# A 90-degree rotation of an 8192 x 8192 matrix: the tile scheduler's unrolled program is replaced by hand-placed buffers, a chunk grid and a PE loop of 64 transposes

## The chip, the cores and the metric

The kernel runs on one core of a Trainium2 chip. The core has five engines that matter here: TensorE (PE, which also does the transposes), VectorE (DVE), ScalarE (ACT), GpSimd (POOL) and SyncE (SP, which here only issues transfers). Sixteen DMA engines move data between the device memory (HBM) and the on-chip memory (SBUF); TensorE writes its results to PSUM, from where another engine has to copy them to SBUF. The metric is the time of one execution on the device in microseconds (us), lower is better. Of the kernel before there are three timed runs: 1267.24, 1267.49 and 1268.66 us, median 1267.49 us.

## The reference

```python
def setup_inputs():
    return {
        "x": np.random.randn(8192, 8192).astype(np.float32),
        "k": 1,
    }

def reference(x, k):
    return np.rot90(x, k)
```

Nothing is computed: row `i` of the output is column `8191 - i` of the input. The 268.4 MB of the input are read once and 268.4 MB of output are written once. The work is a transpose of every 128 x 128 block with the columns in reversed order.

## The kernel before

The input is cut into macro tiles of 1024 rows by 4096 columns (`R = 1024`, `W = 4096`): eight row bands with two macro tiles each. The last macro tile is cut in two of 512 rows (`LAST = [4, 4]`). A macro tile is loaded by `load` in eight transfers of 128 rows x 4096 columns (2 MB each, 16 KB in one piece per row), issued on SP's queue (L102). Every landed row block is copied by VectorE in eight copies of 128 x 512 (L108); each copy also reverses the columns inside each 128-wide block, and puts the result in one of 63 small buffers (`r_pool`). A load buffer is free for the next load when its eight copies are done.

`store` then makes the output of a macro tile in eight units of 2 MB. For a unit, TensorE does 32 transposes of 128 x 128 (L148: the chunk is the loaded operand, the identity matrix the other) into two PSUM tiles of 128 x 2048 (two such tiles exist, together all of PSUM). ScalarE copies each PSUM tile to half of an output buffer (L169), and then issues the store of the whole unit on its own queue (L177): 512 output rows, 4 KB of each.

The buffers are pools: two buffers of 16 KB per partition for loads (`a_pool`), three for stores (`o_pool`), 63 chunk buffers of 2 KB. During the first macro tile, when nothing is stored yet, `load` borrows the store buffers too (`loads % 5 >= 2`), so that five loads are under way. Near the end `store` borrows the load buffers (`end and i % 2 == 0`). Two units of the first macro tile (`i in (4, 6)`) and the last unit of all are stored in two halves. The first unit of a macro tile is transposed row block by row block as the chunks arrive; the others block column by block column. The last half macro tile is loaded while the one before it is stored.

The order on each engine's queue, and every wait, comes from the tile scheduler, which derives them from the order of the calls and from the pools. Each engine's program is straight-line code: TensorE's holds 4096 transposes, each with its own load of the operand. Every engine works through its own queue in order; an instruction waits for the semaphores that the scheduler gave it.

Of the kernel before, what the change touches and what calls it, by code (L numbers as in the profile page):

```python
# [2 lines left out]

# [5 lines left out]

P = 128  # L10

R = 1024
RT = R // P
LAST = [4, 4]
W = 4096
CH = 512
F = 4096  # L20
FP = 2048


def whole_reads(nc):

    for fn in nc.m.functions:
        for block in fn.blocks:
            for n, ins in enumerate(block.instructions):
                if not isinstance(ins, mybir.InstDMACopy):
                    continue
                src = ins.ins[0]
                ap = [list(d) for d in src.ap]
                if len(ap) == 3 and ap[2][0] == 1 and ap[1][0] == ap[2][1]:
                    ap = [ap[0], [1, 1], [1, ap[1][1] * ap[2][1]]]
                    block.instructions[n] = copy.replace(  # L40
                        ins,
                        ins=[copy.replace(src, ap=ap)],
                        ant_dge_precooked=False,
                    )


def macro_tiles(N, M):

    tiles = [(r0, RT, c0) for r0 in range(0, N, R) for c0 in range(0, M, W)]
    r0, _, c0 = tiles.pop()  # L50
    for n in LAST:
        tiles.append((r0, n, c0))
        r0 += n * P
    return tiles


@with_exitstack
def kernel(
    ctx: ExitStack,
    tc: tile.TileContext,  # L60
    x: bass.AP,
    k: bass.AP,
    out: bass.AP,
):
    nc = tc.nc
    assert k == 1, f"only k=1 supported, got {k}"
    nc.at_finalize(whole_reads)

    N, M = x.shape
    dt = x.dtype  # L70

    consts = ctx.enter_context(tc.tile_pool(name="consts", bufs=1))
    ident = consts.tile([P, P], dt)
    make_identity(nc, ident)

    a_pool = ctx.enter_context(tc.tile_pool(name="a_pool", bufs=2))
    r_pool = ctx.enter_context(tc.tile_pool(name="r_pool", bufs=63))
    o_pool = ctx.enter_context(tc.tile_pool(name="o_pool", bufs=3))
    psum_pool = ctx.enter_context(
        tc.tile_pool(name="psum", bufs=2, space=bass.MemoryType.PSUM)  # L80
    )

    loads = 0

    def load(r0, rt, c0):

        nonlocal loads
        chunks = {}
        for t in range(rt):


            if loads < RT and loads % 5 >= 2:
                a = o_pool.tile([P, W], dt, tag="o")
            else:
                a = a_pool.tile([P, W], dt, tag="a")  # L100
            loads += 1
            nc.sync.dma_start(  # L102
                out=a[:], in_=x[r0 + t * P : r0 + (t + 1) * P, c0 : c0 + W]
            )
            yield chunks
            for j in range(W // CH):
                ar = r_pool.tile([P, CH // P, P], dt, tag="ar")
                nc.vector.tensor_copy(  # L108
                    out=ar[:],
                    in_=a[:, j * CH : (j + 1) * CH].rearrange(  # L110
                        "r (b m) -> r b m", m=P
                    )[:, :, ::-1],
                )
                chunks[t, j] = ar
            yield chunks

    def store(r0, rt, c0, chunks, end):

        rows = rt * P
        PW = 1
        while 2 * PW * rows <= FP:
            PW *= 2
        G = PW
        while 2 * G * rows <= F:
            G *= 2
        for i, g0 in enumerate(range(0, W // P, G)):  # L130
            if end and i % 2 == 0:
                ot = a_pool.tile([P, F], dt, tag="a")
            else:
                ot = o_pool.tile([P, F], dt, tag="o")
            o = ot[:, : G * rows].rearrange("m (g f) -> m g f", g=G)

            lead = r0 == 0 and c0 == 0 and i in (4, 6)
            S = PW if lead or (end and r0 + rows == N and g0 + G == W // P) else G  # L140


            ps = {}

            def transposes(t, ws):
                for w in ws:
                    g = g0 + w
                    nc.tensor.transpose(  # L148
                        ps[w // PW][:, PW - 1 - w % PW, t * P : (t + 1) * P],
                        chunks[t, g * P // CH][:, g % (CH // P), :],  # L150
                        ident,
                    )

            def psum_tile(h):
                pt = psum_pool.tile([P, FP], mybir.dt.float32, tag="ps")
                ps[h] = pt[:, : PW * rows].rearrange("m (g f) -> m g f", g=PW)

            if i == 0 and (rt == RT or r0 + rows < N):
                for h in range(G // PW):
                    psum_tile(h)  # L160
                for t in range(rt):
                    transposes(t, range(G))
            for h in range(0, G, PW):
                if h // PW not in ps:
                    psum_tile(h // PW)
                    for w in range(h, h + PW):
                        for t in range(rt):
                            transposes(t, [w])
                nc.scalar.copy(o[:, G - PW - h : G - h, :], ps[h // PW])  # L169

                done = h + PW
                if done % S == 0:
                    top = M - c0 - (g0 + done) * P
                    dst = out[top : top + S * P, r0 : r0 + rows].rearrange(
                        "(g m) f -> m g f", g=S
                    )
                    nc.scalar.dma_start(  # L177
                        out=dst, in_=o[:, G - done : G - done + S, :]
                    )
            yield  # L180

    tiles = macro_tiles(N, M)
    *most, before_last, last = tiles
    for m in most:
        *_, chunks = load(*m)
        for _ in store(*m, chunks, False):
            pass


    *_, chunks = load(*before_last)  # L190
    outputs = store(*before_last, chunks, True)
    rows = load(*last)
    for _ in range(2 * last[1] - 1):
        next(rows)
    next(outputs)
    chunks = next(rows)
    for _ in outputs:
        pass
    for _ in store(*last, chunks, True):
        pass  # L200


# [1 line left out]
_INS = ['x', 'k']  # L204
_OUTS = [((8192, 8192), 'float32')]

_NUMBERS = {'k': 1}


# [26 lines left out]
```

## Time and profile before

| | before |
|---|---|
| median of three runs | 1267.49 us |
| the profiled execution: span | 1266.1 us |
| median less span | 1.39 us |
| DMA: moved, mean rate | 537.55 MB, 425 GB/s |
| PE busy (transposes) | 718.2 us, 57% |
| ACT busy (PSUM to SBUF) | 466.7 us, 37% |
| DVE busy (chunk copies) | 355.4 us, 28% |
| granted TensorE clock, mean | 0.762 |

The profile is one execution recorded by the hardware profiler. The span goes from the first to the last recorded instruction. "Busy" is the time in which an engine had at least one instruction under way; register, semaphore and DMA-issuing instructions do not count. A line such as `L169 ACT COPY ot<-pt` names the source line, the engine, the operation and what is written from what. Idle time is given with what ended it: `<-DMA out_dram<-ot` means that a landed store released the engine. The DMA row of the time slices is the mean busy share of the sixteen DMA engines, in tenths.

### The profile page before, as it was taken

The numbers are of one execution on the slowest core, as the hardware profiler recorded it, in microseconds if no ns is written. First come the engines' busy times: TensorE is split into PE (matmuls) and PEld (weight loads), VectorE is DVE, ScalarE is ACT, GpSimd is POOL, SyncE is SP. The second block draws the span as 40 slices with busy tenths as digits, with TensorE's granted clock in tenths as the row PEclk, the third lists the DMA queues.
The fourth block names the chain that finished last, engine by engine and source line by source line (L and its number), as shares of the span: only waits on it lengthen the run. The fifth ranks groups of instructions, "written<-read, shape, count | busy, mean of one in ns | idle before, by whom it ended". The sixth has DMA issues, their size and how long they took to land.

```text
span 1266.1 us, 10392 instructions
## 1 busy us (share of the span) xinstructions
PE 718.2 (57%) x4096; PEld 678.6 (54%) x4096; DVE 355.4 (28%) x1024; ACT 466.7 (37%) x257; POOL 0.7 (0%) x6
## 2 busy tenths in 40 slices
PE   1554565556656665556555665555655656556673
PEld 1543455555555555456554655555655655556562
DVE  4423223222232223222232223322232222322210
ACT  0432433433333333343334333343333433343363
POOL 0000000000000000000000000000000000000000
PEclk9977877777776777867778678677686686776797
DMA  9999999999999999999999999999999999999997
GB/s 399 426 428 430 428 429 427 430 429 429 429 429 429 430 428 427 430 429 430 428 430 428 429 429 428 430 428 428 430 430 428 429 429 428 428 428 428 427 399 328
DMA packets 37345, 537.55 MB, mean 425 GB/s; under 512 B 4144, under 2 KB 4144, under 8 KB 4144
## 3 DMA queue, kind: packets, MB, share of 16 engines
q10 hardware_dynamic: 18864, 268.44, 50.0%
q1 hardware_dynamic: 18432, 268.44, 49.7%
q8 instruction: 32, 0.52, 0.2%
q14 instruction: 17, 0.14, 0.0%
HBM read 268.44 MB, written 268.44 MB: 424 GB/s over the span
## 4 chain that ended last, share of the span: by engine, by line
DMA 82%; ACT 14%; PE 1%; issue 1%; ACTq 1%; DVE 0%; SPq 0%
DMA out_dram<-ot 79%; ACT ot L169 14%; DMA a<-in_x_dram 3%; PE pt L148 1%; ACTq L177 0%; DVE ar L108 0%; ACTq L169 0%; SPq L102 0%
## 5 line engine op out<-in xcount | busy, mean ns | idle before, releaser
L148 PE MATMUL pt<-ident,ar 128*128 128x128 f32 x4096 | 718.2, 356 | 528.0 <-ACT ot L169 487.6
L148 PEld LDWEIGHTS pt<-ident,ar 128*128 128x128 f32 x4096 | 678.6, 191 | 567.4 <-ACT ot L169 521.4
L169 ACT COPY ot<-pt 128x2048 f32<-128x2048 f32 x256 | 465.4, 1869 | 756.7 <-DMA out_dram<-ot 727.0
L108 DVE COPY ar<-a 128x512 f32<-128x512 f32 x1024 | 355.4, 421 | 861.1 <-DMA a<-in_x_dram 524.0
L169 ACT ACT_TABLE_LOAD x1 | 1.3, 1283 | 25.5 <-DVE ar L108 25.5
masks.py:199 POOL TENSOR_SCALAR_AFFINE_SELECT ident<-ident 128x128 f32<-128x128 f32 x1 | 0.3, 292 | 0.1
masks.py:197 POOL MEMSET ident<- 128x128 f32 x1 | 0.2, 204 | 0.3 <-POOLq L217 0.3
L217 POOL MEMSET const-bfloat16-1.0<- 128x1 bf16 x1 | 0.1, 102 | 0.0
L217 POOL MEMSET const-uint8-127<- 128x1 uint8 x1 | 0.1, 102 | 0.0
L217 POOL MEMSET const-float32-0.0<- 128x1 f32 x1 | 0.1, 99 | 0.2 <-issue 0.2
L217 POOL MEMSET const-float32-1.0<- 128x1 f32 x1 | 0.1, 99 | 0.0
## 6 DMA issues: line engine op xcount, KB each, us to landing
a<-in_x_dram SPq DMA_DIRECT2D x128, 2048.0 KB, 16.8
out_dram<-ot ACTq DMA_DIRECT2D x125, 2048.0 KB, 25.5
out_dram<-ot ACTq DMA_DIRECT2D x6, 1024.0 KB, 27.3
```

The costliest lines, as they stand in the source:

```text
L108: nc.vector.tensor_copy(out=ar[:], in_=a[:, j * CH : (j + 1) * CH].rearrange("r (b m) -> r b m", m=P)[:, :, ::-1],)
L148: nc.tensor.transpose(ps[w // PW][:, PW - 1 - w % PW, t * P : (t + 1) * P], chunks[t, g * P // CH][:, g % (CH // P), :], ident,)
L169: nc.scalar.copy(o[:, G - PW - h : G - h, :], ps[h // PW])
L217: nc = _bacc.Bacc("TRN2", target_bir_lowering=False, num_devices=1)
```

## The change

The kernel is written without the tile scheduler. All buffers have fixed addresses and all semaphores are written out.

- There are four 16 KB buffers (`bufs`). Loads use all four during the first macro tile and then buffers 0 and 1; stores use buffers 2 and 3, and all four for the last eight units. So there are two buffers for loads and two for stores, where there were two and three.
- The 63 chunk buffers become one grid of 8 x 8 chunks of 128 x 512 (`grid`, 128 KB per partition). VectorE first copies a landed row block whole (128 x 4096, in order) into a row or a column of the grid (`place`). For an output unit it then gathers, four times, the eight 128 x 128 blocks of one block column, with reversed columns, into one of two stages of 4 KB per partition (`stage`). When a unit's four gathers are done, its eight chunks of the grid are free, and VectorE places the row block that came eight loads later there; so rows and columns of the grid change roles from one macro tile to the next.
- TensorE runs a loop: 64 iterations of 64 transposes from the two stages to fixed PSUM addresses. Before each group of eight it waits for a full stage (`s_full`), before every second group also for a free half of PSUM (`s_free`). After each group it raises `s_pe`, which frees the stage.
- ScalarE copies each half of PSUM and then waits for its own copy (`s_act`) before it gives the half back. It issues every unit's store whole. The macro tiles are all of 1024 rows, and no store is split.
- A `Block` puts a barrier of all engines before and after this part.

```diff
-R = 1024
-RT = R // P
-LAST = [4, 4]
-W = 4096
-CH = 512
-F = 4096
-FP = 2048
+R = 1024
+T = R // P
+W = 4096
+G = 4
+J = W // (G * P)
+CH = G * P
+F = G * R
+LOOP = 8
+PAIR = 2
...
-    a_pool = ctx.enter_context(tc.tile_pool(name="a_pool", bufs=2))
-    r_pool = ctx.enter_context(tc.tile_pool(name="r_pool", bufs=63))
-    o_pool = ctx.enter_context(tc.tile_pool(name="o_pool", bufs=3))
...
+    macros = [(r0, c0) for r0 in range(0, N, R) for c0 in range(0, M, W)]
+    n_out = len(macros) * J
+    n_load = len(macros) * T
+
+    with tc.tile_critical():
+        ident = nc.alloc_sbuf_tensor("ident", [P, P], dt)
+        bufs = [nc.alloc_sbuf_tensor(f"buf{i}", [P, F], dt) for i in range(4)]
+        grid = nc.alloc_sbuf_tensor("grid", [P, T * J * CH], dt)
+        stage = [nc.alloc_sbuf_tensor(f"stage{i}", [P, R], dt) for i in range(2)]
+        ps = nc.alloc_psum_tensor("ps", [P, 4 * R], mybir.dt.float32)
...
+        def load_buf(m):
+            return m % 4 if m < T else m % 2
+
+        def out_buf(n):
+            return 2 + n % 2 if n < n_out - J else (2 + n) % 4
+
+        def slots(t, kk):
+            g = grid[:].rearrange("p (a b c) -> p a b c", a=T, b=J)
+            return g[:, t, :, :] if kk % 2 == 0 else g[:, :, t, :]
+
+        def column(j, kk):
+            g = grid[:].rearrange("p (a b c) -> p a b c", a=T, b=J)
+            return g[:, :, j, :] if kk % 2 == 0 else g[:, j, :, :]
...
+            @block.sync
+            def _(e):
+                last = {}
+                for m in range(n_load):
+                    b = load_buf(m)
+                    if b in last:
+                        e.wait_ge(s_copy, last[b] + 1)
+                    last[b] = m
+                    r0, c0 = macros[m // T]
+                    r0 += m % T * P
+                    e.dma_start(
+                        out=bufs[b][:], in_=x[r0 : r0 + P, c0 : c0 + W]
+                    ).then_inc(s_land[b], 16)
+
+            @block.vector
+            def _(e):
+                def place(m):
+                    b = load_buf(m)
+                    e.wait_ge(s_land[b], land_wait[m])
+                    e.tensor_copy(
+                        out=slots(m % T, m // T),
+                        in_=bufs[b][:].rearrange("p (j c) -> p j c", c=CH),
+                    ).then_inc(s_copy, 1)
+
+                for t in range(T):
+                    place(t)
+                for n in range(n_out):
+                    kk, j = divmod(n, J)
+                    for w in range(G):
+                        g = n * G + w
+                        if w == 0:
+                            e.wait_ge(s_copy, T * (kk + 1))
+                        if g >= 2:
+                            e.wait_ge(s_pe, g - 1)
+                        e.tensor_copy(
+                            out=stage[g % 2][:].rearrange("p (t c) -> p t c", c=P),
+                            in_=column(j, kk)[:, :, w * P : (w + 1) * P][:, :, ::-1],
+                        ).then_inc(s_full, 1)
+                    if n + T < n_load:
+                        e.drain()
+                        place(n + T)
+
+            @block.tensor
+            def _(e):
+                turns = e.alloc_register("turns")
+                e.wait_ge(s_id, 2)
+                e.reg_mov(turns, n_out * G // LOOP)
+                with e.While(lambda: e.snap(turns) > 0):
+                    for b in range(LOOP):
+                        if b % PAIR == 0:
+                            e.wait_ge(s_free, 1).then_inc(s_free, -1)
+                        e.wait_ge(s_full, 1).then_inc(s_full, -1)
+                        at = (b // PAIR % 2 * PAIR + PAIR - 1 - b % PAIR) * R
+                        for t in range(T):
+                            i = e.transpose(
+                                ps[:, at + t * P : at + (t + 1) * P],
+                                stage[b % 2][:, t * P : (t + 1) * P],
+                                ident[:],
+                            )
+                        i.then_inc(s_pe, 1)
+                    e.reg_sub(turns, turns, 1)
+
+            @block.scalar
+            def _(e):
+                stored = [0] * 4
+                e.sem_inc(s_free, 2)
+                for n in range(n_out):
+                    kk, j = divmod(n, J)
+                    b = out_buf(n)
+                    if stored[b]:
+                        e.wait_ge(s_store[b], stored[b])
+                    else:
+                        e.wait_ge(
+                            s_copy, 1 + max(m for m in range(n_load) if load_buf(m) == b)
+                        )
+                    for h in range(0, G, PAIR):
+                        p = (n * G + h) // PAIR
+                        e.wait_ge(s_pe, n * G + h + PAIR)
+                        at = p % 2 * PAIR * R
+                        to = (G - PAIR - h) * R
+                        e.copy(
+                            bufs[b][:, to : to + PAIR * R], ps[:, at : at + PAIR * R]
+                        ).then_inc(s_act, 1)
+                        e.wait_ge(s_act, p + 1).then_inc(s_free, 1)
+                    r0, c0 = macros[kk]
+                    top = M - c0 - (j + 1) * G * P
+                    e.dma_start(
+                        out=out[top : top + G * P, r0 : r0 + R].rearrange(
+                            "(g m) f -> m g f", g=G
+                        ),
+                        in_=bufs[b][:].rearrange("m (g f) -> m g f", g=G),
+                    ).then_inc(s_store[b], 16)
+                    stored[b] += 16
+                for b in range(4):
+                    e.wait_ge(s_store[b], stored[b])
```

## The prediction

> **What bounds the kernel now.** I read the page first (slices, queues, chain), then the waits, then timelines of one unit in the middle, the start and the end, and last the DMA share in short windows. One unit is one 2 MB load and one 2 MB store.
>
> ```profile
> span 1266.1 us, 10392 instructions
> ...
> DMA  9999999999999999999999999999999999999997
> GB/s 399 426 428 430 428 429 427 430 429 429 429 429 429 430 428 427 430 429 430 428 430 428 429 429 428 430 428 428 430 430 428 429 429 428 428 428 428 427 399 328
> ...
> q8 instruction: 32, 0.52, 0.2%
> ...
> DMA 82%; ACT 14%; PE 1%; issue 1%; ACTq 1%; DVE 0%; SPq 0%
> DMA out_dram<-ot 79%; ACT ot L169 14%; DMA a<-in_x_dram 3%; PE pt L148 1%; ACTq L177 0%; DVE ar L108 0%; ACTq L169 0%; SPq L102 0%
> ...
> L148 PE MATMUL pt<-ident,ar 128*128 128x128 f32 x4096 | 718.2, 356 | 528.0 <-ACT ot L169 487.6
> ...
> L169 ACT COPY ot<-pt 128x2048 f32<-128x2048 f32 x256 | 465.4, 1869 | 756.7 <-DMA out_dram<-ot 727.0
> L108 DVE COPY ar<-a 128x512 f32<-128x512 f32 x1024 | 355.4, 421 | 861.1 <-DMA a<-in_x_dram 524.0
> ```
>
> The DMA engines are full in 39 of 40 slices at about 428.6 GB/s, so a unit's 4.19 MB take 9.79 us. Every engine idles more than half the span, and its idle time ends with a DMA or with somebody who waited for one. The chain shows the same: stores and the ACT copies between them, with loads running underneath.
>
> ```profile
> ACT ot L169 <- DMA out_dram<-ot: 727.0, 118, 11.0
> DVE ar L108 <- DMA a<-in_x_dram: 524.0, 82, 10.2
> PE pt L148 <- ACT ot L169: 487.6, 128, 9.2
> ```
>
> The second view gives total wait, count and the longest. Third, the last steady units, with start and length of each piece:
>
> ```profile
> 1166.88 3.63 ACT L169 COPY ot<-pt 128x2048 f32<-128x2048 f32 x2 [6.20 <-DMA out_dram<-ot]
> 1168.81 6.65 PE L148 MATMUL pt<-ident,ar 128*128 128x128 f32 x32 [3.38 <-ACT ot L169]
> 1174.27 2.78 DVE L108 COPY ar<-a 128x512 f32<-128x512 f32 x8 [7.06 <-DMA a<-in_x_dram]
> ```
>
> In 9.8 us ACT works 3.6, PE 6.65 (its slowest row), DVE 2.8. Only a moment in which the DMA engines have nothing queued costs time. Such moments are at the ends: first and last, the windows (PE, PEld, DVE, ACT, POOL busy; clock; DMA share; GB/s) and three timeline rows:
>
> ```profile
> 45.00:50.00 5.00, 3.85 (x18) 3.85 (x19) 2.78 (x9) 3.00 (x3) 0.00 (x0) 1.00 1.01 429
> 50.00:55.00 5.00, 4.79 (x36) 4.55 (x35) 2.27 (x8) 3.60 (x2) 0.00 (x0) 1.00 1.01 426
> ...
> 1208.00:1210.00 2.00, 1.28 (x9) 0.89 (x9) 0.00 (x0) 1.92 (x2) 0.00 (x0) 0.75 0.86 356
> 1210.00:1212.00 2.00, 2.00 (x10) 2.00 (x11) 0.00 (x0) 0.00 (x0) 0.00 (x0) 0.50 0.87 369
> ...
> 1216.00:1218.00 2.00, 2.00 (x21) 1.96 (x20) 0.49 (x2) 1.33 (x2) 0.00 (x0) 1.00 0.50 213
> ```
>
> ```profile
> 43.02 2.77 DVE L108 COPY ar<-a 128x512 f32<-128x512 f32 x8 [2.08 <-DMA a<-in_x_dram]
> ...
> 47.90 0.64 ACTq L177 DMA_DIRECT2D out_dram<-ot  x1
> ...
> 1224.15 3.74 PE L148 MATMUL pt<-ident,ar 128*128 128x128 f32 x32 [0.59 <-ACT ot L169]
> ```
>
> Where loads give way to stores (45 to 55 us) the share stays 1.01: the first store was issued before the loads ran out. At the other end about 2 x (0.14 + 0.13 + 0.50) = 1.5 us are lost.
>
> **The change, part by part.** The sum goes against the profiled span, 1266.1 us; the median lies 1.39 above it, and I carry that over.
>
> *Middle: 0.* DVE now copies everything twice. Neither shape is in the trace. Upper bounds: a placed row block costs no more than the eight copies it replaces (2.77), a gather of 1024 elements no more than two copies of 512 (0.69); lower bounds are half of these, if fixed costs were half of a copy. I take the uppers, whose operand forms are nearest. DVE then works 2.77 + 4 x 0.69 = 5.5 of 9.8 us. The added waits, counted from a store landing (0): ACT copies one half until 1.9, the other until 3.8, and issues the store at 3.9. PE's groups of eight (6.65 / 4 = 1.66) follow the freed halves and end at 3.6, 5.2, 6.9 and 8.5. DVE's third and fourth gathers wait for the first two groups and end at 4.3 and 5.9, and behind them in DVE's queue stands the placing, 5.9 to 8.7, which releases SP's next load. Behind the placing wait the next unit's gathers, and for them PE; but PSUM holds a finished unit, so PE isn't needed before 9.8 + 1.9. From issue to first packet the packet records show 1.0 us (first load, idle DMA) to 3.2 (first store, busy DMA). The next store's packets thus come by 7.1, the previous store lasts until 9.8: two store buffers suffice with 2.7 to spare. The next load's come by 11.9, so the load before must land at 2.1 or later; up to about 7 does no harm either. In that window neither queue runs dry. What covers all this is PE's 4 us and DVE's 7 us of idle per unit; without that cover, each us is paid 128 times.
>
> *Start: +3.5 (0 to 5.5).* Ten loads alone fill the DMA to about 51.2 (1.7 + 10 x 4.9 + gaps). Before, TensorE transposed as chunks arrived, and the first store left at 47.90. Now the first gather waits until the eighth block is placed: 43.02 + 2.77 + 0.69 = 46.5. PE is slow there, 0.214 us a transpose in the window from 45 us (3.85 / 18), so two groups end at 48.3 and 50.0. The fourth gather ends at 50.7, the placing behind it at 53.5; only then can load 10 go, with packets at 54.5 to 56.7. The store comes later still: the activation table load (1.28 us, formerly at 25.5, off the path) now stands behind the first PSUM half, so copies end at 53.2 and 55.1. The gap is 3.3 to 5.5; with the lower DVE bounds, 0 to 1.9. I take 3.5.
>
> *Barriers: +1.4 (0.6 to 3.0).* The Block adds a barrier at each end. SP's waits show 0.7 us for the one at the start and 0.6 at the end; the last landing to the span's end is 1.5. Two of 0.7.
>
> *Instruction fetches: -2.0 (-4.0 to -1.2).* The queue of 32 packets of 16 KB is 8192 instructions of 64 bytes, exactly 4096 transposes and as many operand loads. A loop needs none of them after the first pass. They last 1.0 us each, 31.8 / 16 = 2.0 us of every DMA engine; at the mean rate 1.2; their lengths repeat every eight, so if eight engines carry them, four each, 4.0.
>
> *Tail: +1.5 (-1.6 to +4.8).* Until unit 121 stores have two buffers, and after the last load they run alone, 4.92 us each. From a landing to the first packet of that buffer's next store: 3.9 + 1.0 to 3.2, so 4.9 to 7.1. Units 119 to 121 leave 0 to 2.1 us idle each; I take 1.0, three times, less the 1.5 that the tail loses already. Then four buffers serve, and the pace is ACT's 3.7 + 0.6 to 1.1 of issue, under 4.92; PE needs 3.74 by the row at 1224.15, with the gathers (0.69) behind the other stage's group (0.94). The unsplit stores and the dropped half macro tiles change no bytes.
>
> The Trainium skill, "TensorE: Matmul & The Clock Gate", Part 4, says that the full clock does not engage for transposes and gives about 275 ns for one inside a kernel. By that a unit would take PE 8.8 us and the tail's eight units would lose 31 us. The row at 1224.15 shows 117 ns at a granted clock of 1.00, and I go by the row.
>
> Sum: 3.5 + 1.4 - 2.0 + 1.5 = +4.4; 1266.1 + 4.4 + 1.39 = 1271.9. The bounds together give 1262.5 to 1281.
>
> **The rivals.**
>
> 1. *The loop fetches its code again each turn.* 64 turns of one or two packets instead of 32 packets: +2 to +6 on the DMA where I have -2, so +4 to +8. PE would also stall up to 4.2 us a turn (3.2 to the first packet, 1.0 to move it): hidden in the middle by 4 us of idle per unit, in the tail 4 turns x (4.2 - 1.2) = up to +12. About 1284. For: every row of before is straight-line code. Against: the body is some 145 instructions, under the 256 that one packet holds. In the Trainium skill, "Runtime: NRT & Kernel Launch", Instruction fetch mechanics, a taken branch stalls on a fetch when its target lies outside the two 16 KB pages held; no run here shows it yet.
>
> 2. *Not slower: the fetches make the late DMA engine.* In the packet records the sixteen parts of the last store land over 6.3 us, and every buffer waits for its latest engine. If the fetches cause that whole lag, removing them gives -6.3, not -2.0, and the time is 1267.6. It decides from a gain of 3.9 on (1270.0). For: lengths repeating every eight. Against: four packets explain only 4.0.
>
> 3. *The queues run dry in the middle.* If a landing to the next first packet takes longer than the cover, both queues empty at once, and 0.2 us a unit is +26: about 1298. Against: 2.7 us to spare above.
>
> 4. *DVE at half speed.* If both shapes ran at twice my uppers, 2 x 5.5 = 11.1 a unit bounds the kernel: 128 x 1.3 more at least, 1434. Against: the chunk copy reads the same reversed 128-runs.
>
> **How the numbers follow.** Under 0.2% (2.5 us) a measurement of this kernel can't tell from no change, so slower starts at 1270.0 and faster below 1265.0. Mine 0.68 (inside it slower 0.39, same 0.22, faster 0.07; its own range 1265 to 1278), rival 1 0.10, rival 2 0.12 (same 0.08, faster 0.03, slower 0.01), rival 3 0.07, rival 4 0.03. Together: faster 0.10, same 0.30, slower 0.60. The range 1265 to 1285 takes in rival 1 and leaves out the faster cases and rivals 3 and 4, 0.2 in all.
>
> **What would show it.** Right: the DMA row full in the middle at 428 to 430 GB/s; a dip of 3 to 4 us between 51 and 57; the first store issued near 55; the instruction queue at a few packets; PE's wait for ACT still its largest. Wrong: 64 or more instruction packets (rival 1), landings within 2 us of each other (rival 2), a middle below 425 GB/s (rival 3), placings above 4 us (rival 4).

## The result, and the profile after

The changed kernel takes 1274.01 us (median of four runs, 1272.91 to 1274.94), the kernel before beside it 1267.55 us. The ratio is 1.0048, with a 95% interval of 1.0034 to 1.0062: slower by about 6.5 us. The profiled execution took 1274.23 us with a span of 1272.4 us, 6.3 us more than before's (1266.1). Time less span is 1.7 to 1.8 us in these four runs, and 1.7 to 1.9 in all runs of before that list both; the 1.39 of the table takes the span of one execution from the median of others. So practically all of the difference lies inside the span.

The page of the changed kernel, with the rows that answer to those shown of before:

```profile
span 1272.4 us, 11079 instructions
...
DMA  9999999999999999999999999999999999999989
GB/s 396 379 430 429 430 429 429 430 430 428 429 431 429 430 429 430 429 430 430 426 426 425 414 424 423 425 421 416 429 426 417 430 430 429 429 429 422 419 361 387
...
q1 hardware_dynamic: 18432, 268.44, 50.1%
q10 hardware_dynamic: 18432, 268.44, 49.7%
q14 instruction: 14, 0.11, 0.0%
...
DMA 74%; ACT 20%; issue 1%; ACTq 1%; PE 0%
...
L163 PE MATMUL ps<-ident,stage 128*128 128x128 f32 x4096 | 722.3, 357 | 537.1 <-PEq L160 536.6
...
L189 ACT COPY buf<-ps 128x2048 f32<-128x2048 f32 x256 | 477.9, 1867 | 733.2 <-DMA out_dram<-buf 712.5
L143 DVE COPY stage<-grid 128x1024 f32<-128x1024 f32 x512 | 343.1, 690 | 592.3 <-PE ps L163 591.0
L128 DVE COPY grid<-buf 128x4096 f32<-128x4096 f32 x128 | 293.6, 2294 | 38.0 <-DMA buf<-in_x_dram 26.8
...
buf<-in_x_dram SPq DMA_DIRECT2D x128, 2048.0 KB, 14.5
out_dram<-buf ACTq DMA_DIRECT2D x128, 2048.0 KB, 15.7
```

Four things stand here. The queue of instruction packets (q8, 32 packets before) is gone. The second slice, 32 to 64 us, falls to 379 GB/s, where before had 426: that is the start. The DMA row is full from there to the tail, and yet the slices from 600 to 1000 us fall as low as 414 GB/s, in a stretch in which before never went under 427. And the last two rows say how long before its landing a transfer was issued: 14.5 us for a load and 15.7 us for a store. In the kernel before, the same rows of its page read:

```profile
a<-in_x_dram SPq DMA_DIRECT2D x128, 2048.0 KB, 16.8
out_dram<-ot ACTq DMA_DIRECT2D x125, 2048.0 KB, 25.5
```

A transfer's own turn is 9.8 us when loads and stores alternate. What is above that is its lead, the time that it lay in the queue behind the one before it: 15.7 us for a store before, 5.9 us now, and 7.0 and 4.7 us for a load.

The start in short windows (PE, PEld, DVE, ACT, POOL busy; clock; DMA share; GB/s), and the two timeline rows that explain it:

```profile
50.00:52.00 2.00, 1.98 (x13) 1.74 (x11) 1.90 (x2) 1.99 (x2) 0.00 (x0) 1.00 0.62 262
52.00:54.00 2.00, 0.86 (x8) 0.89 (x9) 1.60 (x3) 1.88 (x2) 0.00 (x0) 1.00 0.60 123
54.00:56.00 2.00, 2.00 (x19) 1.77 (x18) 1.49 (x3) 1.14 (x2) 0.00 (x0) 1.00 0.73 303
```

```profile
50.10 2.29 DVE L128 COPY grid<-buf 128x4096 f32<-128x4096 f32 x1
...
54.61 0.65 ACTq L195 DMA_DIRECT2D out_dram<-buf  x1
```

The packets of the ten loads end between 51 and 52.4 us, engine by engine. The placing that lets load 10 go ends at 52.4, its first packet comes at 53.4, and the first store is issued at 54.61 (before: 47.90) and has its first packet at 59.4. Counted in bytes moved, the kernel is 3.5 us behind before at 120 us.

The middle, first the kernel before and then the changed kernel, the same 20 us (same columns):

```profile
700.00:720.00 20.00, 11.83 (x65) 11.36 (x64) 5.55 (x16) 7.27 (x4) 0.00 (x0) 0.67 1.01 431
```

```profile
700.00:720.00 20.00, 12.54 (x64) 12.12 (x64) 9.77 (x10) 7.73 (x5) 0.00 (x0) 0.67 1.00 415
```

The share hardly moves (1.01 to 1.00) and 4% of the rate is gone. The trace's packet records show where: the 16 KB packets of the loads take 620.8 ns in the mean, 613.3 before, and 425 of them take over 700 ns (85 before). By the bytes of loads and stores the kernel is 2.4 us behind before at 560 us, 5.2 at 840 and 7.8 at 1200. That counts all sixteen DMA engines together; what it means for the time is taken up with the run on two store buffers.

The tail, where the loads have ended, in the same columns, and ACT's queue there:

```profile
1214.00:1216.00 2.00, 1.15 (x7) 1.19 (x8) 0.00 (x0) 1.88 (x2) 0.00 (x0) 0.76 0.54 229
1216.00:1218.00 2.00, 2.00 (x11) 2.00 (x10) 0.69 (x1) 0.49 (x1) 0.00 (x0) 0.50 0.52 221
...
1222.00:1224.00 2.00, 1.69 (x16) 1.72 (x16) 1.35 (x3) 1.37 (x1) 0.00 (x0) 1.00 0.35 147
1224.00:1226.00 2.00, 2.00 (x19) 1.72 (x17) 1.38 (x3) 1.50 (x1) 0.00 (x0) 1.00 0.86 360
```

```profile
1212.64 3.85 ACT L189 COPY buf<-ps 128x2048 f32<-128x2048 f32 x2 [6.04 <-DMA out_dram<-buf]
1216.59 0.56 ACTq L195 DMA_DIRECT2D out_dram<-buf  x1
1219.51 3.86 ACT L189 COPY buf<-ps 128x2048 f32<-128x2048 f32 x2 [3.02 <-DMA out_dram<-buf]
1223.47 0.56 ACTq L195 DMA_DIRECT2D out_dram<-buf  x1
```

Twice nothing is queued while ACT fills a half-empty pair of buffers: 2 x (0.46 + 0.48) + 2 x (0.65 + 0.14) = 3.5 us, with smaller gaps 4.7 us, where before lost 1.65. Between 1206 and 1240 us alone the DMA engines are idle 4.6 us (before 1.5). From the last landing of the last load to the last landing of all, before needed 51.4 us and the changed kernel 54.6. Against that, the sixteen parts of the last store now land within 0.6 us of each other, before over 6.3 us.

### The profile page after: what moved, and what is told of

It reads as the page before. It is cut to its first block, busy times and chain, and to the rows that moved or that the text cites. A ratio compares the mean times of both kernels' runs of the same rounds, so it can differ in the third digit from the quotient of the medians.

```text
span 1272.4 us, 11079 instructions
## 1 busy us (share of the span) xinstructions
PE 722.3 (57%) x4096; PEld 686.5 (54%) x4096; DVE 627.9 (49%) x640; ACT 479.2 (38%) x257; POOL 0.7 (0%) x6
## 2 busy tenths in 40 slices
DMA packets 36878, 537.00 MB, mean 422 GB/s; under 512 B 4096, under 2 KB 4096, under 8 KB 4096
## 4 chain that ended last, share of the span: by engine, by line
DMA 74%; ACT 20%; issue 1%; ACTq 1%; PE 0%
DMA out_dram<-buf 74%; ACT buf L189 20%; ACTq L195 0%; PE ps L163 0%; ACTq L192 0%; ACT L189 0%; ACTq L186 0%
## 5 line engine op out<-in xcount | busy, mean ns | idle before, releaser
L163 PE MATMUL ps<-ident,stage 128*128 128x128 f32 x4096 | 722.3, 357 | 537.1 <-PEq L160 536.6
L163 PEld LDWEIGHTS ps<-ident,stage 128*128 128x128 f32 x4096 | 686.5, 192 | 572.7 <-issue 571.9
L189 ACT COPY buf<-ps 128x2048 f32<-128x2048 f32 x256 | 477.9, 1867 | 733.2 <-DMA out_dram<-buf 712.5
L143 DVE COPY stage<-grid 128x1024 f32<-128x1024 f32 x512 | 343.1, 690 | 592.3 <-PE ps L163 591.0
L128 DVE COPY grid<-buf 128x4096 f32<-128x4096 f32 x128 | 293.6, 2294 | 38.0 <-DMA buf<-in_x_dram 26.8
## 6 DMA issues: line engine op xcount, KB each, us to landing
buf<-in_x_dram SPq DMA_DIRECT2D x128, 2048.0 KB, 14.5
out_dram<-buf ACTq DMA_DIRECT2D x128, 2048.0 KB, 15.7
```

What stands on the lines that cost most here:

```text
L128: e.tensor_copy(out=slots(m % T, m // T), in_=bufs[b][:].rearrange("p (j c) -> p j c", c=CH),).then_inc(s_copy, 1)
L143: e.tensor_copy(out=stage[g % 2][:].rearrange("p (t c) -> p t c", c=P), in_=column(j, kk)[:, :, w * P : (w + 1) * P][:, :, ::-1],).then_in ...
L163: i = e.transpose(ps[:, at + t * P : at + (t + 1) * P], stage[b % 2][:, t * P : (t + 1) * P], ident[:],)
L189: e.copy(bufs[b][:, to : to + PAIR * R], ps[:, at : at + PAIR * R]).then_inc(s_act, 1)
```

## The experiments

Two theories stood at first: the loss is at the ends (start and tail), or it is in the middle. When single edits at the ends moved little, the second round asked whether the two store buffers lose time by themselves, whether the DMA engines drift apart by themselves, and the third, what makes them drift.

**Fetches.** The loop is written out as straight-line code.

```diff
-                with e.While(lambda: e.snap(turns) > 0):
+                for turn in range(n_out * G // LOOP):
```

> The changed kernel with TensorE's program written out in full instead of the loop; nothing else differs. Theory of the prediction: the 32 instruction packets of 16 KB come back, 31.8 us over 16 DMA engines, so 1 to 3 us slower than the changed kernel's 1274.0 (1275 to 1277), and the landing spread of the last store stays small. Rival, the loop itself holds TensorE up: then this run is faster than the changed kernel by 2 us or more.

Measured: 1274.5 us, ratio to before 1.0058 (1.0045 to 1.0072). The page has the packets back:

```profile
q8 instruction: 34, 0.56, 0.2%
```

Against the changed kernel that is 0.5 us by the medians and 1.3 by the ratios, and the intervals overlap. Inside the span nothing is lost: the spans of the five runs have a median of 1271.9 us, those of the changed kernel's four 1272.2. What is longer lies outside it (time less span is 2.5 to 3.0 us here, 1.7 to 1.8 there). So no gain from the missing fetches is seen inside the span, where 2.0 us were forecast, and they were not what made the last store land over 6.3 us: with them in, it lands over 1.6 us here.

**The tail.** The last eight units take the buffers in the other order, the free load buffers first.

```diff
-            return 2 + n % 2 if n < n_out - J else (2 + n) % 4
+            return 2 + n % 2 if n < n_out - J else n % 4
```

> The changed kernel with the last eight units' buffers in the order 0, 1, 2, 3 instead of 2, 3, 0, 1, so that units 120 and 121 need not wait for the stores of 118 and 119. Theory: the idle DMA time between 1222 and 1236 us in the changed kernel (1.84 and 0.73 us of the mean engine) goes: 2 to 3 us faster, 1271 to 1272. Rival, the tail is paced by something else (the gathers, ScalarE): no change.

Measured: 1273.56 us, 1.0049 (1.0035 to 1.0062). The expectation missed. The windows show that a gap at 1234 us went (0.74 of the DMA share before the edit, 0.93 with it), while the one at 1222 us is deeper (0.35 before the edit, 0.04 with it). The large gap at 1222 to 1224 belongs to unit 119, the last one before the four buffers serve: its copies began at 1219.51, when the store two units earlier landed, and the edit does not touch it.

**The activation table.** ACT makes one small copy early, so that the table is loaded long before the first PSUM half.

```diff
                 stored = [0] * 4
+                e.wait_ge(s_id, 2)
+                e.copy(warm[:], ident[:, :1]).then_inc(s_warm, 1)
+                e.wait_ge(s_warm, 1)
                 e.sem_inc(s_free, 2)
```

> The changed kernel with a copy of one column on ScalarE before anything else, so that the activation table load no longer stands behind the first half of PSUM. Theory: the first store leaves 1.3 us earlier (53.3 instead of 54.6 us); the kernel gains 0.5 to 1.3 us, 1272.7 to 1273.5. Rival, the gap at the start is closed by load 10 alone, whose first packet comes at 53.4: no change.

Measured: 1273.39 us, 1.0049 (1.0036 to 1.0063). The start's windows stay as they were:

```profile
50.00:52.00 2.00, 2.00 (x13) 1.92 (x11) 1.90 (x2) 1.25 (x1) 0.00 (x0) 1.00 0.62 262
52.00:54.00 2.00, 1.01 (x10) 0.88 (x9) 1.61 (x3) 1.80 (x1) 0.00 (x0) 1.00 0.51 115
```

The median lies in the theory's range, 0.6 us under the changed kernel's, but the ratio is practically the same and the intervals overlap. The first store was issued at 54.17 instead of 54.61, and the gap did not close: load 10 ends it (first packet at 53.4 in both), and load 10 waits for the placing behind the fourth gather.

**Stores in halves.** Each half of an output buffer gets its own store and its own wait, so that ACT can refill a half as soon as it has landed.

```diff
+                        hb = 2 * b + h // PAIR
+                        if stored[hb]:
+                            e.wait_ge(s_store[hb], stored[hb])
...
-                    e.dma_start(
-                        out=out[top : top + G * P, r0 : r0 + R].rearrange(
-                            "(g m) f -> m g f", g=G
-                        ),
...
+                        e.dma_start(
+                            out=out[up : up + PAIR * P, r0 : r0 + R].rearrange(
+                                "(g m) f -> m g f", g=PAIR
+                            ),
...
+                        ).then_inc(s_store[hb], 16)
```

> The changed kernel with every store split in its two halves of 1 MB, each with its own semaphore and issued as soon as its copy is done; the buffers are the same 32 KB. Theory A (one late DMA engine sets the pace, so the 5 us of bytes that the changed kernel falls behind between 640 and 1000 us cost nothing at the end): gains at the start (first store 2 us earlier) and in the tail only, 3 to 5 us, 1269 to 1271. Theory B (the two store buffers slow the middle, and that adds to the end): the middle comes back to 428 GB/s or more as well and the gain is 8 us or more, 1266 or below.

Measured: 1297.66 us, 1.0224 (1.0201 to 1.0247). Both theories missed; it is the slowest of all. Its queues and its rates:

```profile
GB/s 397 383 430 426 423 421 415 430 420 400 423 399 421 424 392 427 422 409 415 406 418 394 411 421 419 417 427 416 414 417 398 407 419 423 416 407 427 401 414 362
...
q1 hardware_dynamic: 18432, 268.44, 50.4%
q10 hardware_dynamic: 36864, 268.45, 49.2%
...
buf<-in_x_dram SPq DMA_DIRECT2D x128, 2048.0 KB, 12.3
out_dram<-buf ACTq DMA_DIRECT2D x256, 1024.0 KB, 17.9
```

The store queue now has twice the packets, of 8 KB each. In the packet records load and store packets are served in turn: where both are queued, 17 load packets and 16 store packets start in a microsecond (medians). So loads, still with 16 KB a packet, move two bytes for each byte of the stores. A load then lands early and its queue is empty until the next: its issue-to-landing time falls from 14.5 to 12.3 us, and 1402 load packets take over 700 ns. The edit made worse what it was to mend, and so said nothing for or against the tail. That the packets' size makes the loss is read from these records: the edit also doubled the number of stores and of waits, and no run has the one without the other.

**Two store buffers in the kernel before.** The pool of output buffers shrinks from three to two, and with it the number of loads under way at the start from five to four; scheduler, straight-line code, chunk buffers and tail stay.

```diff
-    o_pool = ctx.enter_context(tc.tile_pool(name="o_pool", bufs=3))
+    o_pool = ctx.enter_context(tc.tile_pool(name="o_pool", bufs=2))
...
-            if loads < RT and loads % 5 >= 2:
+            if loads < RT and loads % 4 >= 2:
```

> The kernel before with two store buffers instead of three (and four instead of five loads in flight in the first macro tile); scheduler, unrolled TensorE program, chunk buffers and the split ends stay. Theory A (the buffer count alone makes the changed kernel's middle fall behind): the DMA rate falls below 427 GB/s somewhere after 600 us, more long load packets, and 3 to 6 us are lost against 1267.4 (1270 to 1273). Theory B (the loss comes from the chain of gathers and placings): 1267 to 1269, middle unchanged.

Measured: 1271.07 us, 1.0029 (1.0019 to 1.0040), against 1267.25 us for before: 3.8 us.

```profile
GB/s 399 426 426 430 428 428 428 430 429 428 428 428 429 429 423 429 429 429 428 422 426 429 429 430 429 428 421 425 426 428 429 429 429 422 427 425 429 428 359 374
...
out_dram<-ot ACTq DMA_DIRECT2D x125, 2048.0 KB, 15.8
```

The store's issue-to-landing time is the changed kernel's (15.8 against 15.7), and the rate dips in the middle too (423, 422, 421, 425, 422), though less (414 to 417 there). By bytes it is 0.4 us behind before at 560 us and 2.7 at 1200. All signs of theory A came, its time as well. But the dips are not where the time goes. A buffer comes back, and the kernel ends, with the last of a transfer's sixteen parts. So here is, from the semaphore events of one trace each, by how many us the n-th load and the n-th store have landed whole later than before (minus: earlier):

| | 30th | 60th | 90th | 115th | 128th |
|---|---|---|---|---|---|
| before, two store buffers: loads | 3.6 | 3.5 | 2.9 | 2.5 | 3.0 |
| stores | -3.2 | -3.2 | -3.2 | -3.4 | 2.6 |
| changed kernel: loads | 0.8 | 0.5 | 1.8 | 2.2 | 2.7 |
| stores | 3.7 | 3.6 | 6.0 | 6.4 | 5.9 |
| changed, straight-line code: loads | 1.8 | 1.7 | 2.6 | 2.0 | 1.9 |
| stores | 3.6 | 3.6 | 5.0 | 4.5 | 5.3 |

With two store buffers the loads run a little later than before and the stores a little earlier, and neither loses anything from the 30th to the 115th, dips or not: taken together they are about even with before until then, and 2.6 us behind at the end. The loss comes in the tail, where stores run alone and ACT has to refill a buffer in time (windows as above):

```profile
1214.00:1216.00 2.00, 1.06 (x5) 1.06 (x6) 0.00 (x0) 2.00 (x2) 0.00 (x0) 0.50 0.45 188
1216.00:1218.00 2.00, 2.00 (x11) 1.80 (x10) 1.29 (x4) 0.66 (x1) 0.00 (x0) 0.50 0.37 156
...
1222.00:1224.00 2.00, 1.76 (x16) 1.73 (x16) 0.00 (x0) 1.96 (x2) 0.00 (x0) 1.00 0.39 164
1224.00:1226.00 2.00, 1.98 (x18) 1.73 (x16) 0.00 (x0) 1.37 (x1) 0.00 (x0) 1.00 0.61 262
```

The whole tail in one window, for before, the changed kernel and this run:

```profile
1206.00:1240.00 34.00, 26.40 (x214) 24.36 (x215) 3.39 (x10) 25.46 (x14) 0.00 (x0) 0.95 0.96 400
1206.00:1240.00 34.00, 24.39 (x182) 22.20 (x181) 19.57 (x24) 19.86 (x12) 0.00 (x0) 0.92 0.86 365
1206.00:1240.00 34.00, 25.41 (x189) 23.63 (x188) 5.64 (x16) 21.13 (x13) 0.00 (x0) 0.86 0.86 363
```

With unrounded shares the DMA engines are idle 4.6 us here, 4.6 in the changed kernel and 1.5 before. So the run shows that two store buffers alone cost 3.8 us, over half of the loss, and its trace puts them in the tail. The changed kernel's own lateness in the middle, 1.4 us (loads) to 2.7 (stores) between the 30th and the 115th, is not explained by it.

**The split ends.** The kernel before with whole macro tiles only, no load running under the last stores.

```diff
-LAST = [4, 4]
+LAST = [8]
...
-    *most, before_last, last = tiles
-    for m in most:
+    for m in tiles:
         *_, chunks = load(*m)
-        for _ in store(*m, chunks, False):
+        for _ in store(*m, chunks, m is tiles[-1]):
...
```

> The kernel before with the last macro tile whole (1024 rows) and stored after its load, instead of two halves whose load and store overlap; everything else as before. Prices the tail alone: the theory that the split bought about 3 us in the tail gives 1270 to 1271; if only the buffer count matters there, 1267 to 1268.

Measured: 1267.01 us, 0.9996 (0.9987 to 1.0005). Giving up the halved last macro tile costs nothing.

**Transfers alone.** Loads and stores as in the changed kernel, two buffers each, and no engine at work; then with four buffers each.

```diff
-L = 2
-S = 2
+L = 4
+S = 4
```

> No computation: the same 128 loads and 128 stores of 2 MB, two buffers each, stores of a constant, no dependence between the two (the rotation is left out). Theory (one DMA engine is late by itself): the landing spread grows over the run to several us although nothing but DMA runs, the unit pace of the last engine is about 9.85 us, and the time is 1258 to 1266. Rival (lateness is made by instruction fetches or by the engines' waits): spread under 1 us throughout and a pace of 9.76, 1250 to 1256.

> The same with four load and four store buffers. Theory: deeper queues let the early engines run further ahead, the spread grows beyond that of two buffers, and the time is within 2 us of it, because the late engine's own work sets the end. Rival (depth keeps the rate up): 3 us or more faster than with two.

Measured: 1257.17 us with two and 1257.62 us with four (two runs each). The first one's page:

```profile
span 1255.3 us, 329 instructions
...
GB/s 384 430 430 430 430 430 430 429 431 427 432 429 430 430 431 430 429 431 428 432 428 430 430 430 430 430 431 428 432 427 431 429 430 430 430 430 429 431 427 394
```

The sixteen parts of a transfer land within 1.1 us of each other to the end with two buffers, and within 1.6 with four. The theory of the first run is dead: nearly the rival's spread came, and a time 1 us above its range. The second run is within 2 us of the first, as its theory had it. So depth is worth nothing to the transfers as such, and no DMA engine is late by itself. The floor for these bytes is 10 us under the kernel before.

**Start and tail together.** The changed kernel with a third stage, the early table load and the other tail order; the loop then has 12 groups, and the last eight groups are written out behind it.

```diff
-LOOP = 8
+LOOP = 12
...
-        stage = [nc.alloc_sbuf_tensor(f"stage{i}", [P, R], dt) for i in range(2)]
+        stage = [nc.alloc_sbuf_tensor(f"stage{i}", [P, R], dt) for i in range(3)]
...
-                        if g >= 2:
-                            e.wait_ge(s_pe, g - 1)
+                        if g >= 3:
+                            e.wait_ge(s_pe, g - 2)
```

> The changed kernel with three gather stages instead of two (so that the placing of row block 8, and with it load 10, does not wait for the second group of transposes), the activation table load moved ahead, and the last eight units' buffers in the order 0, 1, 2, 3. Theory: the 2.0 us of idle DMA between 50 and 54 us, and about as much again in long load packets until 60 us, go, and 0.5 us in the tail: 3 to 4.5 us faster than the changed kernel, 1269.5 to 1271. Rival (the two store buffers decide alone, and what is won at the start is lost again behind the late DMA engines): 1273 or more.

Measured: 1271.0 us, 1.0029 (1.0017 to 1.0040); 3.0 us less than the changed kernel. That is the upper end of the theory's range. The gap of the start is nearly closed, idle 0.5 us instead of 2.1:

```profile
50.00:52.00 2.00, 2.00 (x17) 1.87 (x16) 2.00 (x4) 1.54 (x2) 0.00 (x0) 1.00 0.96 344
52.00:54.00 2.00, 1.68 (x16) 1.44 (x14) 1.73 (x4) 1.73 (x1) 0.00 (x0) 1.00 0.80 295
```

With three stages the fourth gather waits for one group fewer, the placing behind it comes earlier, and load 10's first packet comes at 51.8 us instead of 53.4. The three edits went in together; the two tried alone had brought 0.5 and 0.6 us by the medians, within their intervals. What remains over before is 3.7 us. By bytes 1.8 of them are there at 120 us (3.5 in the changed kernel), and in the tail the DMA engines are idle 4.4 us between 1206 and 1240, nearly as in the changed kernel (4.6; before 1.5). That 3.7 is close to the 3.8 of two store buffers is no proof that it is the same loss.

**What makes the DMA engines drift.** The transfers alone, and beside them the work of one engine, on buffers that no transfer touches: DVE's four gathers and a placing per load; ACT's two PSUM copies per store; PE's 32 transposes per load.

```diff
+                for m in range(n_load):
+                    e.wait_ge(s_land[m % L], 16 * (m // L + 1))
+                    for w in range(4):
+                        e.tensor_copy(
+                            out=stage[w][:].rearrange("p (t c) -> p t c", c=P),
...
+                    e.tensor_copy(out=grid[:], in_=src[:, :F])
...
```

> The transfers alone with two buffers each, and beside every landed load one placing copy and four gathers on VectorE between buffers of their own (the rotation is left out). Theory (VectorE's traffic in SBUF makes some DMA engines late): the landing spread grows to 3 us or more and the time to 1260 or more. Otherwise 1257 to 1258 with a spread of about 1.

```diff
+                    for h in range(2):
+                        e.copy(
+                            side[:, h * 2 * R : (h + 1) * 2 * R],
+                            ps[:, h * 2 * R : (h + 1) * 2 * R],
+                        ).then_inc(s_act, 1)
+                        e.wait_ge(s_act, 2 * n + h + 1)
```

> The transfers alone with two buffers each, and ahead of every store two copies of 128 x 2048 from PSUM to a buffer of their own on ScalarE (the rotation is left out). If ScalarE's writes make the engines late: spread of 3 us or more, 1260 or more, beyond the 4 us by which the first store leaves later. Otherwise 1257 to 1262 with a spread of about 1.

```diff
+                with e.While(lambda: e.snap(turns) > 0):
+                    e.wait_ge(s_tick, 1).then_inc(s_tick, -1)
+                    for b in range(4):
+                        for t in range(T):
+                            e.transpose(
...
```

> The transfers alone with two buffers each, and after every landed load 32 transposes from two fixed stages in a loop on TensorE (the rotation is left out). If TensorE's reads of SBUF make the engines late: spread of 3 us or more and 1260 or more. Otherwise 1257 to 1258.

Measured, with the landing spread of the loads (median of the first and of the last sixteen, from the packet records):

| | us | over transfers alone | spread, first to last loads |
|---|---|---|---|
| transfers alone | 1257.17 | | 0.8 to 1.1 us |
| with ACT | 1259.46 | 2.3 | 1.2 to 2.2 us |
| with DVE | 1260.93 | 3.8 | 0.8 to 4.5 us |
| with PE | 1262.67 | 5.5 | 0.8 to 6.3 us |
| before | 1267.29 | 10.1 | 1.0 to 8.3 us |

The page of the run with PE shows the lateness only at the end, where the early DMA engines have finished and the late one has not:

```profile
GB/s 387 428 431 429 428 432 429 428 432 429 428 432 429 428 431 430 427 432 429 428 432 429 428 431 430 427 432 429 428 431 430 428 430 430 428 431 429 429 430 322
```

The expectations of DVE and PE came, with a spread over 3 us and a time over 1260; with ACT the other case came, 1259.46 us, with a spread of 2.2. Work on DVE or PE makes the sixteen DMA engines unequal, PE's the most, and the three excesses together (11.6 us) are about what the kernel before has; that they add up was not tested. ACT's 2.3 us are mostly another matter: there a store is issued behind two copies, as in the changed kernel, and its trace has 2.2 us of idle DMA at the end. The pace sorts this out: from the 21st to the 121st, a load lands whole every 9.762 us alone, 9.768 with ACT, 9.796 with DVE, 9.813 with PE and 9.846 in the kernel before. By what path an engine's work slows some DMA engines and not others was not tried. A third store buffer in the changed kernel wasn't tried either; with it grid, buffers and stages would take 216 KB a partition, where the kernel before has 206.

## Why the prediction was right, and where not

Right: slower, inside the range, 1271.9 us against 1274.01. The terms of the sum:

- **Start, +3.5: size right, by a partly different way.** 3.5 us behind in bytes at 120 us; first store at 54.61 (forecast 55.1). The placing took 2.294 us, under the upper bound of 2.77; the gather 0.690, on its bound of 0.69. But load 10's packets came at 53.4, before the 54.5 to 56.7 of the forecast, and the DMA engines idle only 2.1 us between 48 and 64. The rest goes behind the gap, where the rate is still low (393 and 254 GB/s from 56 to 60 us); the first store's packets came 4.8 us after its issue, where 3.2 was the most that was taken. That load 10 and not the store ends the gap, as the step had it, is shown by the early table load, which left it as it was, and by the run with a third stage, which nearly closed it.
- **Barriers, +1.4: mis-sized.** SP's first load is issued at 0.96 us (0.74 before), and 2.0 us lie between the last packet and the span's end (1.5 before): +0.7, near the lower bound.
- **Fetches, -2.0: mis-sized.** The packets went, but no run shows a gain from it inside the span (1271.9 us with them, 1272.2 without).
- **Tail, +1.5: mis-sized.** +3.2 us by the landings after the last load, +3.1 by the idle DMA between 1206 and 1240 us, inside the bounds. The mechanism was right: with two buffers the refill after a landing comes too late for a store alone. The gaps had their place: units 118 and 119 lost about 1.9 and 1.6 us where 1.0 each was taken. ACT's pace afterwards was under 4.92, as forecast. The kernel before with two store buffers has the same 4.6 us of idle DMA there.
- **Middle, 0: incomplete, and its price is open.** "Two store buffers suffice with 2.7 to spare": the arithmetic holds for the last DMA engine, since a store issued 3.9 us after a landing leaves 5.9 us of lead, which the page confirms (15.7 - 9.8). What it left out is that a landing is not one moment, though the prediction had such a spread at hand (6.3 us for the last store, used only for the second rival). The sixteen parts of a store land up to 9 us apart in the middle (median of sixteen units 5.6 to 8.5), and the buffer is free only with the last of them. An early DMA engine has moved its share by then and can have nothing of the next transfer queued. Before, with a lead of 15.7 us, the parts of a store drew up to 16.6 us apart, and the rate held. So the lead seems to bound how far the early engines run ahead, and with it the mean rate. That the long load packets are those of early engines starting again from an empty queue is read from the records, not tested apart. But an early engine that waits does not make the last one later: with two store buffers in the kernel before, the dips cost no landing in the middle. The changed kernel did fall 1.4 to 2.7 us back there. The straight-line version, with the same buffers, fell back 0.2 to 0.9 in its trace, and the four spans of the changed kernel differ by 2.1 us among themselves. So the cause of this part stays open; the shorter lead of the loads (4.7 us instead of 7.0) is a candidate that no run tests alone.

Together: start 3.5, barriers 0.7 and tail 3.2 are 7.4 us, more than the 6.3 of the spans, for they count different things (bytes of all engines, landings of the last). What edits show is this: the third stage, the early table load and the other tail order together bring 3.0 us, and two store buffers cost the kernel before 3.8. They may overlap in the tail and are not a sum. That the forecast came within 2.1 us is in part luck: the gain of 2.0 that was not seen and the tail's 1.7 too little made it too low, the barriers' 0.7 too high. And its upper bound was added up wrongly: 5.5 + 3.0 - 1.2 + 4.8 on 1266.1 + 1.39 is 1279.6, not 1281; the range did not hang on it.

The rivals. *The loop fetches again:* dead, there is no packet on that queue in 64 turns. The Trainium skill, "Runtime: NRT & Kernel Launch", Instruction fetch mechanics, has a taken branch stall on a fetch when its target is outside the pages held; this body of some 145 instructions stays inside, and the trace agrees. *The fetches make the late DMA engine:* its sign came, the end spread did go (6.3 to 0.6 us), but not its time. In the middle the parts of a store land 5.6 to 8.5 us apart without any fetch, the unrolled loop with its packets has 1.6 at the end, and the kernel before without the split ends, with its packets and three store buffers, has 2.1. So the end spread goes neither with the fetches nor with the number of store buffers alone; what sets it was not tried. *The queues run dry in the middle:* its sign (slices under 425 GB/s) came, its mechanism and its price did not. It let both queues of all sixteen engines empty in every unit, +26 us; in fact the share of busy DMA is 1.00 in the middle's window, and at most single engines run dry for moments. *DVE at half speed:* dead, 2.29 + 4 x 0.69 = 5.05 us a unit.

The tail's transposes run at 123 ns (32 in 3.93 us at a granted clock of 1.00), where the Trainium skill, "TensorE: Matmul & The Clock Gate", Part 4, gives about 275 ns and no full clock for transposes. The measurement decides, as it did in the prediction.

## What to carry to other kernels

A landing is as late as the latest of sixteen DMA engines, and so is the end of the kernel. The row of the issues gives the lead at a glance (time from issue to landing, less a transfer's own turn). The share of busy DMA does not show a short lead, since it stayed at 1.00 where 4% of the rate was lost. GB/s shows it, but is no price: it counts the early engines with the late one, and in the kernel before with two store buffers it dipped to 421 without a later landing. Before a dip is priced, set side by side when the n-th transfer has landed whole in both kernels. The short lead was paid where the loads had ended and stores ran alone (4.6 us of idle DMA instead of 1.5). And in the one run in which the two queues had packets of different size, 24 us were lost.

## What was not expected of the hardware

- Work on the compute engines, on buffers of their own, slows the transfers: 3.8 us (DVE) and 5.5 (PE) over a floor of 1257.2, and spreads the landings of a load from 1.1 us to 4.5 and 6.3. ACT's work does so little (2.2 us, and 9.768 us a load against 9.762). So even the kernel before is 10 us over what its transfers need.
- In the kernel before the parts of one store land up to 16.6 us apart, more than the 9.8 us of a whole unit.
- Halving the store's packets to 8 KB, with the same bytes and more freedom for ACT, cost 24 us against the changed kernel.
